# Value projection in blocks of four heads through DRAM, in place of blocks of two heads kept on chip, in a two-layer hybrid decoder

## The chip, the cores and the metric

The kernel runs on one core of one Trainium2 chip. The metric is the time of one execution in microseconds (us) on the device; lower is better.

## The reference

The input is x, 1024 tokens by 1024 channels, float32. Two residual layers follow, then a final RMSNorm; every layer is `x = x + mixer(rmsnorm(x))`.

```python
# layer 0: one projection u @ w_in, split into two branches
z, xBC, dt, q, k, v, g = split(u @ w_in)
xBC = silu(causal_dwconv(xBC))              # Mamba-2 branch: 4 groups, 8 chunks of 128 tokens
y_a = rmsnorm((ssd_scan(xs, dt, A, B, C) + xs * D_skip) * silu(z))
# differential attention: 8 heads, two softmax maps each, values 128 wide
w   = softmax(q0 k0 + bias) - lam * softmax(q1 k1 + bias)
y_b = rmsnorm(w @ v) * silu(g)
out = concat(y_a, y_b) @ w_out
# layer 1: gated recurrence (HGRN2), 16 heads of 128
q, f, i, g = split(u @ w_in)                # i are the values of the recurrence
o = gated_linear_recurrence(silu(q), 1 - f, i, log f)
out = (rmsnorm(o) * silu(g)) @ w_out
```

Layer 0 needs 1024 value columns (8 heads of 128), layer 1 needs 2048 (16 heads of 128).

## The kernel before, in words

Matrix products in float32 are made of three products of rounded parts: each operand is split into a high and a low part, and TensorE (PE in the profile) adds high·high, high·low and low·high in PSUM. The normed input of a layer, `u`, lies on chip for the whole layer, 8 high and 8 low tiles of 128 channels by 1024 tokens.

Weights come in blocks of 256 columns by 1024 rows (`wspecs` is the list of blocks in the order of their use). `_wprep` loads a block in two halves into `w_raw` on the SP queue (L126), rounds it on ScalarE (ACT, L132) into `w_hi`, and takes the rest on VectorE (DVE, L133) into `w_lo`. There are two buffers of each, so one block can be made ready while another is in use; `wnext` hands out a block and begins the next.

A projection comes in two forms. `mm_cm` (L174) has the weights stationary and streams 512 tokens per matmul; it makes queries, keys, gates and the scan's inputs. `mm_tm` (L184) has 128 tokens of `u` stationary and streams the weight columns, 256 per matmul; it makes the values, which are wanted with tokens on partitions, and the output projections. Both write a PSUM tile `pj`, of which there are two of one bank each. A `pj` tile is free for the next piece when ACT and DVE have taken its result out.

Values: `v_pieces` takes one weight block (two heads) and makes, in four pieces of 48 matmuls, the two tiles `V` that hold 1024 tokens by 256 value columns; ACT copies each piece out of PSUM (L199). The tag `V` has four buffers, so two pairs of heads fit.

Layer 0 first runs the scan group by group. The order of PE's instructions there is written out by `weave`: the projections of group g+1 are cut into pieces, and behind certain pieces the steps of group g's scan are put. Each of the 8 chunks has a `first` step (transposes; the decay matrix R, tile `G` or `wT`, read from DRAM on SP, L464, shifted on DVE, L482, exponentiated on ACT) and a `second` step two pieces later (L502 to L508). The numbers that `at` gives are the pieces behind which the steps come. In the last group there is no next group; the pieces are the query and key projection of attention head 0 (4), the values of heads 0 and 1 (4) and the gates (4).

Then come 8 attention heads, and in them and in all of layer 1 a scheduler orders each engine's instructions. A head has 8 query blocks i of 128 tokens. `soft(i)` makes two score maps of 128 by 128(i+1) in PSUM tiles `big` (L603), takes their maxima with the bias on DVE (L607 for the last 256 columns, L611 for the rest, L613), exponentials on ACT (L617), and combines the two maps on DVE (L621 to L624). `values(i)` transposes the result (L635, copies L637) and multiplies with `V` (L639). Queries and keys of a head are taken out of `pj` by ACT (L569) and DVE (L570) into `A` tiles; head h+1's are projected beside head h's work. Behind odd heads the next two heads' values are projected, before even heads their gates.

Layer 1 has 16 heads of the recurrence (`hgrn_core`); per head a projection of q and f, then before even heads the gates of two heads, after odd heads the values of the next two.

Of the kernel before, what the change touches and what calls it, by code (L numbers as in the profile page):

```python
# [89 lines left out]
class Net:  # L90
# [23 lines left out]
    def _wprep(self, i):  # L114
# [4 lines left out]
        hi = self.t("w_hi", [P, KT, WB], F32R)  # L119
        lo = self.t("w_lo", [P, KT, WB], F32R)  # L120
        for q in range(2):
            raw = self.t("w_raw", [P, KT // 2, WB])
            k0 = q * (KT // 2)
            o = 0
            for c0, n in cols:
                nc.sync.dma_start(  # L126
                    raw[:, :, o:o + n],
                    src[row0 + k0 * P:row0 + (k0 + KT // 2) * P, c0:c0 + n].rearrange(
                        "(k p) n -> p k n", p=P))
# [57 lines left out]

    def v_pieces(self, u, vs):
        nc = self.nc
        w = self.wnext()  # L190
        for q in range(2):
            v = self.t("V", [P, 4, WB])
            vs.append(v)
            for j2 in range(2):
                pj = self.ps("pj")
                for j in range(2):
                    sl = slice((q * 4 + j2 * 2 + j) * P, (q * 4 + j2 * 2 + j + 1) * P)
                    self.mm_tm(pj[:, j * WB:j * WB + WB], w, [x[:, sl] for x in u[0]], [x[:, sl] for x in u[1]])
                nc.scalar.copy(v[:, 2 * j2:2 * j2 + 2, :], pj.rearrange("p (t n) -> p t n", n=WB))  # L199
                yield  # L200
# [994 lines left out]
```

## Time and profile before

| | |
|---|---|
| median of 3 runs | 2237.67 us (2235.84 to 2238.94) |
| the profiled execution | 2242.69 us |
| its span in the profile | 2240.9 us, so 1.8 us lie outside |
| PE busy | 2178.8 us (97%), 16868 matmuls |
| DVE busy | 1269.9 us (57%) |
| ACT busy | 832.2 us (37%) |
| chain that ended last | PE 51%; first lines: pj L174 24%, pj L184 14% |
| DMA | 169.14 MB, mean 75 GB/s |
| granted TensorE clock, mean | 0.991 of full speed |

The profiled execution is 5.0 us longer than the median of the runs. A busy PE is not PE at its peak: each matmul's end is modelled, and two that follow each other overlap in the rows. The distance from start to start is what one costs.

### The profile page before, as it was taken

Reading aid. Unit: us, or ns where it says so; the run is one execution under the profiler, and the core shown is the slowest. Engines: PE = TensorE matmul, PEld = TensorE weight load, DVE = VectorE, ACT = ScalarE, POOL = GpSimd, SP = SyncE. Lnnn points to the kernel's source line nnn. Section 1 sums busy time; section 2 is a strip of 40 time slices with the busy share of each in tenths; the row PEclk is TensorE's granted clock in tenths of the full one; section 3 lists DMA queues with packets and bytes.
Section 4 is the critical chain, followed back from the end, with each engine's and each line's share of the span. In section 5 each row is a group of like instructions: output and inputs, shape, how many; then the busy total and the mean of one; then the engine's idle time right before and its main releaser. Section 6 shows DMA issues by size and latency. Waiting matters only on the chain.

```text
span 2240.9 us, 40897 instructions
## 1 busy us (share of the span) xinstructions
PE 2178.8 (97%) x16868; PEld 1920.3 (86%) x16868; DVE 1269.9 (57%) x2864; ACT 832.2 (37%) x1903; POOL 188.8 (8%) x216
## 2 busy tenths in 40 slices
PE   6998998899999999999999999999999999999998
PEld 5787776789898988999988989898989898989998
DVE  4765766565656556755453555555555555557444
ACT  4333333234444545644442323232323222324233
POOL 1001111110000000000010010101010101010000
PEclk9999999999999999999999999999999999999999
DMA  4322233332212221525331111111111111125333
GB/s 138 67 84 66 80 85 81 74 81 64 69 36 67 64 69 41 170 66 159 119 104 39 48 48 48 48 48 48 48 48 48 48 49 48 48 67 165 111 103 122
DMA packets 182256, 169.14 MB, mean 75 GB/s; under 512 B 10239, under 2 KB 163233, under 8 KB 182068
## 3 DMA queue, kind: packets, MB, share of 16 engines
q1 hardware_dynamic: 174564, 152.42, 23.1%
q0 software_dynamic: 3280, 9.90, 2.1%
q10 hardware_dynamic: 4224, 4.19, 0.6%
q8 instruction: 132, 2.16, 0.4%
q14 instruction: 56, 0.46, 0.1%
HBM read 132.66 MB, written 25.43 MB: 71 GB/s over the span
## 4 chain that ended last, share of the span: by engine, by line
PE 51%; DMA 1%; ACT 0%; DVE 0%; issue 0%; POOL 0%; POOLq 0%; ACTq 0%
PE pj L174 24%; PE pj L184 14%; PE big L184 5%; PE big L1051 2%; PE big L1139 1%; PE big L1141 1%; PE s L1128 1%; PE big L1093 1%; PE s L1155 1%; PE s L1122 1%; PE big L1087 0%; PE s L159 0%; DMA ey<-yb 0%; DMA th<-in_lvmask 0%; ACT w_hi L132 0%; DVE w_lo L133 0%
## 5 line engine op out<-in xcount | busy, mean ns | idle before, releaser
L174 PE MATMUL pj<-u,w_hi 128*128 128x512 f32 x3072 | 990.0, 400 | 31.3 <-DVE A L233 21.2
L174 PEld LDWEIGHTS pj<-u,w_hi 128*128 128x128 f32 x3072 | 573.4, 190 | 154.7 <-DVE A L233 23.0
L174 PE MATMUL pj<-u,w_lo 128*128 128x512 f32 x1536 | 607.9, 396 | 0.0
L184 PE MATMUL pj<-w_hi,u 128*128 128x256 f32 x2592 | 492.6, 286 | 1.0 <-DVE A L233 1.0
L184 PEld LDWEIGHTS pj<-w_hi,u 128*128 128x128 f32 x2592 | 409.9, 191 | 3.6 <-DVE A L233 1.4
L184 PE MATMUL pj<-w_lo,u 128*128 128x256 f32 x1296 | 368.3, 284 | 0.0
L174 PEld LDWEIGHTS pj<-u,w_lo 128*128 128x128 f32 x1536 | 291.8, 190 | 61.1 <-issue 0.2
L133 DVE TENSOR_TENSOR w_lo<-w_raw,w_hi 128x1024 fp32r<-128x1024 f32 x168 | 206.3, 1251 | 116.9 <-ACT w_hi L132 116.6
L184 PEld LDWEIGHTS pj<-w_lo,u 128*128 128x128 f32 x1296 | 247.8, 191 | 1.0
L132 ACT CAST w_hi<-w_raw 128x1024 fp32r<-128x1024 f32 x168 | 168.1, 1047 | 188.8 <-PE pj L174 107.6
L233 DVE SCALAR_TENSOR_TENSOR A<-th,pj 128x512 f32<-128x512 f32 x80 | 55.1, 689 | 140.9 <-ACT th L232 140.4
L232 ACT ACTIVATE th<-pj 128x512 f32<-128x512 f32 x96 | 57.2, 596 | 208.5 <-PE pj L174 190.8
L617 ACT ACTIVATE p<-p,mx 128x256 f32<-128x256 f32 (+7 forms) x128 | 98.5, 771 | 72.4 <-DVE mx L613 66.4
L148 POOL TENSOR_TENSOR ro<-rs_t,mhalf 128x4 f32<-128x4 f32 x48 | 52.8, 1100 | 682.4 <-DVE rs_t L147 489.1
L603 PE MATMUL big<-A 128*128 128x512 f32 (+3 forms) x384 | 90.3, 352 | 2.6 <-DMA A<-A 1.3
L968 POOL TENSOR_SCALAR A<-th,fN,fB 128x512 f32<-128x512 f32 x32 | 47.6, 1488 | 470.0 <-ACT th L965 470.0
L637 ACT COPY wT<-s 128x512 f32<-128x512 f32 (+2 forms) x96 | 45.8, 477 | 95.8 <-PE s L635 95.1
L639 PE MATMUL s<-V,wT 128*128 128x128 f32 x576 | 79.7, 275 | 0.6 <-ACT wT L637 0.6
L1035 DVE TENSOR_TENSOR A<-A,p 128x512 f32<-128x512 f32 x96 | 65.8, 686 | 23.5 <-PE big L1051 23.0
L639 PEld LDWEIGHTS s<-V,wT 128*128 128x128 f32 x576 | 74.4, 191 | 3.3 <-ACT wT L637 1.1
L1030 DVE TENSOR_TENSOR p<-p,p 128x512 f32<-128x512 f32 x96 | 66.2, 690 | 15.5 <-PE big L1087 6.2
L603 PEld LDWEIGHTS big<-A 128*128 128x128 f32 x384 | 64.5, 189 | 11.3 <-issue 2.3
(330 smaller groups left out, 2977.1 us busy)
## 6 DMA issues: line engine op xcount, KB each, us to landing
w_raw<-in_even_w_in SPq DMA_DIRECT2D x32, 512.0 KB, 4.7
w_raw<-in_odd_w_in SPq DMA_DIRECT2D x64, 256.0 KB, 3.3
w_raw<-in_odd_w_in SPq DMA_DIRECT2D x32, 512.0 KB, 3.9
w_raw<-in_even_w_in SPq DMA_DIRECT2D x48, 256.0 KB, 4.3
w_raw<-in_even_w_out SPq DMA_DIRECT2D x24, 512.0 KB, 4.4
w_raw<-in_odd_w_out SPq DMA_DIRECT2D x24, 512.0 KB, 4.6
A<-A POOLq DMA_DIRECT2D x32, 256.0 KB, 5.5
yo<-ey SPq DMA_DIRECT2D x32, 256.0 KB, 2.0
```

Source lines behind the costliest of these rows:

```text
L132: nc.scalar.copy(hq, raw)
L133: nc.vector.tensor_tensor(lq, raw, hq.bitcast(F32), op=ALU.subtract)
L148: return nc.gpsimd.tensor_tensor(dst, t[:, :n], self.mhalf[:, :n], op=ALU.pow)
L174: nc.tensor.matmul(out, lhsT=ww[:, k, ms], rhs=uu[k][:, sl], start=(n == 0), stop=(n == 3 * KT - 1))
L184: nc.tensor.matmul(out, lhsT=uu[k], rhs=ww[:, k, :], start=(k == 0 and j == 0), stop=(k == KT - 1 and j == 2))
L232: nc.scalar.activation(th, pj, AF.Tanh, scale=0.5)
L233: nc.vector.scalar_tensor_tensor(out, view(th), 1.0, view(pj), op0=ALU.add, op1=ALU.mult)
L603: nc.tensor.matmul(s[:, k0:k0 + kn], lhsT=q[:, isl], rhs=ks[j][:, k0:k0 + kn], start=(j == 0), stop=(j == 1))
L617: nc.scalar.activation(p[:, :n], p[:, :n], AF.Exp, bias=mx, accum_out=z)
L639: nc.tensor.matmul(po[:, i % 4, :], lhsT=wT[:, j * P:j * P + P], rhs=V(j, hh), start=(j == 0), stop=(j == i))
L1030: nc.vector.tensor_tensor(q, q, bc(t0, [P, L // (2 * h), h]), op=ALU.mult)
L1035: nc.vector.tensor_tensor(k, k, bc(halves(Ts[h], 1)[1], [P, L // (2 * h), h]), op=ALU.mult)
```

## The change

Values are projected for four heads at once. A value block is now two weight blocks of 512 rows by 512 columns, which together fill both weight buffers; a matmul streams 512 columns (L187). For each pair of 128-token tiles two `pj` tiles are filled: in the first and the last pair in the order tile 0 and tile 1 with the first weight block, then both with the second; in the others tile by tile. ACT copies a tile into a staging `V` tile of two token tiles, SP stores it to the DRAM tensor `v_d`, and `v_load` reads two tiles of 1024 tokens by 256 columns back for each pair of heads. Value blocks stand in layer 0 in the scan's last group (heads 0 to 3) and at head 3 (heads 4 to 7), in layer 1 at heads 0, 3, 7 and 11. Since a value block is now 8 pieces, the last scan group has 16 pieces, and its steps stand at 1.5 + 1.6c in place of 1.5 + c. Line numbers move: L174 is now L176, L184 is L187, L482 is L502, L570 is L590, L603 is L623, L635 is L655, L639 is L659.

```diff
 def _wprep(self, i):
...
-        hi = self.t("w_hi", [P, KT, WB], F32R)
-        lo = self.t("w_lo", [P, KT, WB], F32R)
+        wid = sum(n for _, n in cols)
+        kt = KT * WB // wid
+        hi = self.t("w_hi", [P, kt, wid], F32R)
+        lo = self.t("w_lo", [P, kt, wid], F32R)
...
-    def v_pieces(self, u, vs):
+    def v_pieces(self, u, v_d, hb):
         nc = self.nc
-        w = self.wnext()
+        i = self.wpos
+        self.wpos += 2
+        self._wprep(i)
+        self._wprep(i + 1)
+        ws = self.wtiles[i], self.wtiles[i + 1]
+        for t in range(0, NT, 2):
+            pas = [self.ps("pj") for _ in range(2)]
+            order = ((0, 0), (1, 0), (0, 1), (1, 1)) if t in (0, NT - 2) else ((0, 0), (0, 1), (1, 0), (1, 1))
+            for j, kq in order:
+                sl = slice((t + j) * P, (t + j) * P + P)
+                self.mm_tm(pas[j], ws[kq], *([x[:, sl] for x in z[4 * kq:4 * kq + 4]] for z in u),
+                           first=kq == 0, last=kq == 1)
+                if t == NT - 2 and j == 1:
+                    self._wprep(i + 2 + kq)
+                if kq == 1:
+                    if j == 0:
+                        v = self.t("V", [P, 2, 512])
+                    nc.scalar.copy(v[:, j], pas[j])
+                    if j:
+                        nc.sync.dma_start(v_d[t * P:(t + 2) * P, hb * 512:hb * 512 + 512].rearrange(
+                            "(t p) n -> p t n", p=P), v)
+                    yield
+    def v_load(self, v_d, pair):
+        vs = []
         for q in range(2):
             v = self.t("V", [P, 4, WB])
+            self.nc.sync.dma_start(v, v_d[q * 512:q * 512 + 512, pair * WB:pair * WB + WB].rearrange(
+                "(t p) n -> p t n", p=P))
             vs.append(v)
...
+    values = lambda c0, hb: [(W, r0, [(c0 + hb * 512, 512)]) for r0 in (0, 512)]
...
-                pieces = chain(att_pieces(S, u, nxt), S.v_pieces(u, vs), S.gate_pieces(u, ("G", "bt"), sg))
-                steps = ssd_steps(S, g, tiles, ya, lambda c: 1.5 + c, 2)
+                pieces = chain(att_pieces(S, u, nxt), S.v_pieces(u, v_d, 0), S.gate_pieces(u, ("G", "bt"), sg))
+                steps = ssd_steps(S, g, tiles, ya, lambda c: 1.5 + 1.6 * c, 2)
...
         elif h < 7:
-            Vn = S.proj_v(u)
+            if h == 3:
+                run(S.v_pieces(u, v_d, 1))
+            Vn = S.v_load(v_d, h // 2 + 1)
...
         elif h < 15:
-            Vn = S.proj_v(u)
+            if h % 4 == 3:
+                run(S.v_pieces(u, v_d, h // 4 + 1))
+            Vn = S.v_load(v_d, h // 2 + 1)
```

**Place 1: the beginning of the value block in the scan's last group.** PE before: `pj_3118` is the first piece of values (48 matmuls), `pj_3207` the second; the rows with `big` and `s1` between them are scan steps.

```order
L508 MATMUL big_3070<-G_2956,p0_2963 64x128 x4
...
L470 MATMUL s1_3085<-ident_71,A_2417 128x128
L184 MATMUL pj_3118<-w_hi_2869,u_76 128x256 [waits DVE_49,PE_49]
L184 MATMUL pj_3118<-w_lo_2870,u_76 128x256
...
L184 MATMUL pj_3118<-w_hi_2869,u_91 128x256
L502 MATMUL big_3168<-A_2418,p0_2963 128x128 [waits Activation_49]
...
L508 MATMUL big_3168<-G_3023,p0_3030 64x128 x4
...
L470 MATMUL s1_3191<-ident_71,A_2417 128x128
L184 MATMUL pj_3207<-w_hi_2869,u_76 128x256 [waits DVE_49,PE_49]
```

PE now: `pj_3100` and `pj_3101` are the first two token tiles; 12 matmuls of 512 columns with the first weight block go to each, then the second weight block (`w_hi_3090`) begins.

```order
L528 MATMUL big_3071<-G_2957,p0_2964 64x128 x4
L187 MATMUL pj_3100<-w_hi_2870,u_77 128x512 [waits DVE_49,PE_49]
L187 MATMUL pj_3100<-w_lo_2871,u_77 128x512
...
L187 MATMUL pj_3100<-w_hi_2870,u_88 128x512
L187 MATMUL pj_3101<-w_hi_2870,u_77 128x512 [waits DVE_49,PE_49]
L187 MATMUL pj_3101<-w_lo_2871,u_77 128x512
...
L187 MATMUL pj_3101<-w_hi_2870,u_88 128x512
L187 MATMUL pj_3100<-w_hi_3090,u_81 128x512 [waits Activation_49]
```

The second `pj` tile of the block is asked for after 12 matmuls of 512 columns now; before, after 48 of 256 columns and two scan steps.

DVE before, the same place: `pj_3041` is the last piece of the query and key projection, `G_3189` a decay matrix R that SP reads from DRAM.

```order
L570 SCALAR_TENSOR_TENSOR A_2992<-pj_3041,A_2992 64x512 [waits Activation_49]
L532 COPY o_3081<-big_3070 128x2x128 [waits DMAHW6_49,Activation_49]
L514 TENSOR_TENSOR p0_3030<-p0_2963,ph_511 128x256
L482 TENSOR_SCALAR G_3189<-G_3189,ph_510 128x128 [waits DMAHW6_49]
L480 TENSOR_TENSOR bt_3090<-s1_3085,triu_132 128x128 [waits Activation_49]
L482 TENSOR_SCALAR G_3189<-G_3189,ph_510 128x128 x3
L570 SCALAR_TENSOR_TENSOR A_2993<-pj_3041,A_2993 64x512 [waits Activation_49]
L485 TENSOR_TENSOR wT_3083<-wT_3083,bt_3090 128x512 [waits DVE_49]
```

DVE now: `pj_3024` is that last piece, and its second row (into `A_2994`) is what frees the bank for `pj_3101`; `G_3221` is the R.

```order
L590 SCALAR_TENSOR_TENSOR A_2993<-pj_3024,A_2993 64x512 [waits Activation_49]
L500 TENSOR_TENSOR p0_3060<-s1_3055,triu_133 128x128 [waits Activation_49]
L552 COPY o_3082<-big_3071 128x2x128 [waits DMAHW6_49,Activation_49]
L534 TENSOR_TENSOR p0_3060<-p0_2964,ph_512 128x256
L502 TENSOR_SCALAR G_3221<-G_3221,ph_511 128x128 [waits DMAHW6_49]
L502 TENSOR_SCALAR G_3221<-G_3221,ph_511 128x128 x3
L505 TENSOR_TENSOR G_3053<-G_3053,p0_3060 128x512 [waits DVE_49]
L590 SCALAR_TENSOR_TENSOR A_2994<-pj_3024,A_2994 64x512 [waits Activation_49]
```

In both lists the second take-out of that piece stands behind the rows on an R; now a multiplication with the R before (`G_3053`) stands ahead of it too.

**Place 2: attention head 4, query blocks 3 to 6.** PE before: `big` are score maps, `s1` the values' products, `pj_7109` and `pj_7159` pieces of the values of heads 6 and 7.

```order
L603 MATMUL big_6580<-A_6275,A_6215 128x512 [waits DVE_49,PE_49]
L603 MATMUL big_6580<-A_6335,A_6215 128x512
L184 MATMUL pj_7109<-w_hi_6859,u_84 128x256
...
L184 MATMUL pj_7109<-w_hi_6859,u_83 128x256
L639 MATMUL s1_6521<-V_5609,wT_6554 128x128 [waits Activation_49]
...
L603 MATMUL big_6605<-A_6274,A_6214 128x512 [waits DVE_49,PE_49]
...
L184 MATMUL pj_7109<-w_lo_6860,u_83 128x256
...
L184 MATMUL pj_7159<-w_lo_6860,u_78 128x256
L639 MATMUL s1_6521<-V_5609,wT_6596 128x128 [waits Activation_49]
...
L603 MATMUL big_6666<-A_6274,A_6214 128x512 [waits DVE_49]
...
L184 MATMUL pj_7159<-w_hi_6859,u_86 128x256
...
L603 MATMUL big_6713<-A_6274,A_6214 128x512 [waits DVE_49]
```

PE now, from query block 3 to the next projection (`pj_7315`, the third piece of head 5's queries and keys); pieces 1 and 2 of that projection are `pj_7255` and `pj_7284`, ahead of this stretch.

```order
L623 MATMUL big_6418<-A_6123,A_6063 128x512 [waits DVE_49,PE_49]
...
L623 MATMUL big_6429<-A_6124,A_6064 128x512 [waits DVE_49,PE_49]
...
L623 MATMUL big_6454<-A_6123,A_6063 128x512 [waits DVE_49,PE_49]
...
L659 MATMUL s1_6370<-V_5666,wT_6403 128x128 [waits Activation_49]
...
L623 MATMUL big_6467<-A_6124,A_6064 128x512 [waits DVE_49,PE_49]
...
L623 MATMUL big_6515<-A_6123,A_6063 128x512 [waits DVE_49]
...
L659 MATMUL s1_6370<-V_5666,wT_6485 128x128 [waits Activation_49]
...
L623 MATMUL big_6562<-A_6123,A_6063 128x512 [waits DVE_49]
...
L623 MATMUL big_6618<-A_6123,A_6063 128x512 [waits DVE_49,PE_49]
...
L623 MATMUL big_6631<-A_6124,A_6064 128x512 [waits DVE_49,PE_49]
...
L659 MATMUL s1_6546<-V_5666,wT_6593 128x128 x4
L176 MATMUL pj_7315<-u_77,w_hi_6708 128x512 [waits DVE_49]
```

From the last matmul of `pj_7284` to the first of `pj_7315` PE has no projection: 40 score matmuls (query blocks 2 to 7, both maps), 21 transposes of weights, 19 value products and 4 transposes of the tail lie between. DVE's rows that free `pj_7255` stand here:

```order
L644 SCALAR_TENSOR_TENSOR p0_6521<-p1_6534,rr_6541,p0_6521 128x768 [waits DVE_49]
L643 RECIPROCAL rr_6588<-z0_6573 128x1 [waits Activation_49]
L627 ISA p1_6581,mx_6580<-big_6575,cm_6315 128x256 [waits DVE_49,PE_49]
...
L631 ISA p1_6581,mf_6583<-big_6575,far_851 128x640
...
L590 SCALAR_TENSOR_TENSOR A_7253<-pj_7255,A_7253 64x512 [waits Activation_49]
L590 SCALAR_TENSOR_TENSOR A_7253<-pj_7284,A_7253 64x512 [waits Activation_49]
...
L633 TENSOR_SCALAR mx_6580<-mx_6580,mf_6583 128x1 [waits DVE_49]
L590 SCALAR_TENSOR_TENSOR A_7254<-pj_7255,A_7254 64x512 [waits DMASW2_49,DMASW1_49,Activation_49]
```

They stand behind the maxima of query block 6 (`big_6575`) and the combination of block 5 (`p0_6521`).

## Rows read from the trace of the kernel before

**Rows 1.** Windows: us, busy time and count per engine, granted clock, DMA.

```profile
480.00:860.00 380.00, 380.00 (x2297) 338.11 (x2296) 216.24 (x682) 185.80 (x456) 24.22 (x34) 1.00 0.23 57
860.00:910.00 50.00, 47.76 (x278) 41.33 (x277) 35.14 (x96) 27.61 (x61) 3.70 (x6) 0.97 0.34 91
1168.00:2040.00 872.00, 871.11 (x8235) 755.36 (x8236) 478.31 (x941) 262.00 (x652) 78.71 (x59) 1.00 0.17 51
```

**Rows 2.** Timeline, TensorE, layer 1: start, us, instruction (L184, 256 columns).

```profile
1242.63 0.40 PE L184 MATMUL pj<-w_hi,u 128*128 128x256 f32 x2
...
1246.23 0.28 PE L184 MATMUL pj<-w_hi,u 128*128 128x256 f32 x1
```

**Rows 3.** Timeline, TensorE, layer 0, scan stage (L174, 512 columns).

```profile
132.38 0.62 PE L174 MATMUL pj<-u,w_hi 128*128 128x512 f32 x2
...
136.49 0.62 PE L174 MATMUL pj<-u,w_hi 128*128 128x512 f32 x2
```

**Rows 4.** Waits of TensorE from 390 to 410 us: total, times, longest.

```profile
PE pj L174 <- DVE A L570: 8.0, 1, 8.0
```

**Rows 5.** Window behind that wait, columns as in rows 1.

```profile
406.00:410.00 4.00, 4.00 (x11) 3.08 (x11) 0.03 (x1) 0.00 (x0) 0.95 (x2) 0.51 0.10 33
```

**Rows 6.** Timeline, SP queue (DMA issues), beginning of the value block in layer 0.

```profile
420.43 0.37 SPq L464 DMA_DIRECT2D G<-acs_d  x1
```

**Rows 7.** Timeline, VectorE, the same place.

```profile
426.66 0.29 DVE L482 TENSOR_SCALAR G<-G,ph 128x128 f32<-128x128 f32 x1 [2.09 <-DMA G<-acs_d]
...
427.77 0.69 DVE L570 SCALAR_TENSOR_TENSOR A<-pj,A 64x512 fp32r<-64x512 f32 x1
```

**Rows 8.** Timeline, TensorE, the same place.

```profile
420.89 0.36 PE L184 MATMUL pj<-w_hi,u 128*128 128x256 f32 x1
...
428.85 0.36 PE L184 MATMUL pj<-w_hi,u 128*128 128x256 f32 x1
```

**Rows 9.** DMA issues of the page: count, KB, median us to landing.

```profile
w_raw<-in_odd_w_in SPq DMA_DIRECT2D x32, 512.0 KB, 3.9
...
G<-acs_d SPq DMA_DIRECT2D x22, 256.0 KB, 4.9
```

**Rows 10.** Windows, attention head 4, value block (L184) alone.

```profile
764.00:792.00 28.00, 20.26 (x155) 19.14 (x154) 1.00 0.27 67
```

**Rows 11.** Groups of VectorE, 460 to 905 us: busy us, mean ns.

```profile
L570 DVE SCALAR_TENSOR_TENSOR A<-pj,A 64x512 fp32r<-64x512 f32 x55 | 37.9, 689 | 26.2 <-ACT A L569 25.2
...
L607 DVE CUSTOM_DVE_ANT_0 p<-big,cm 128x256 f32<-128x256 f32 x42 | 17.5, 421 | 15.8 <-PE s L635 14.6 <-PE big L603 1.1
L613 DVE TENSOR_SCALAR mx<-mx,mf 128x1 f32<-128x1 f32 x72 | 12.5, 208 | 0.2
...
L607 DVE DVE_READ_ACCUMULATOR2_ANT mx<- 128x1 f32 x98 | 8.1, 83 | 0.0
...
L611 DVE CUSTOM_DVE_ANT_0 p<-big,far 128x640 f32<-128x640 f32 x12 | 9.8, 820 | 0.0
...
L624 DVE SCALAR_TENSOR_TENSOR p<-p,rr,p 128x768 f32<-128x768 f32 x6 | 6.1, 1019 | 0.2
...
L624 DVE SCALAR_TENSOR_TENSOR p<-p,rr,p 128x384 f32<-128x384 f32 x6 | 3.7, 619 | 0.2
...
L611 DVE CUSTOM_DVE_ANT_0 p<-big,far 128x128 f32<-128x128 f32 x12 | 3.4, 286 | 0.0
```

**Rows 12.** Windows in attention head 5, columns as in rows 1.

```profile
880.00:888.00 8.00, 6.41 (x40) 5.33 (x38) 7.31 (x18) 3.91 (x9) 1.67 (x3) 0.99 0.35 82
861.00:892.00 31.00, 28.78 (x151) 24.15 (x151) 23.25 (x67) 16.48 (x39) 2.67 (x4) 0.94 0.25 73
```

**Rows 13.** Timeline, TensorE, in that stretch (values, 128 columns).

```profile
882.35 1.50 PE L639 MATMUL s<-V,wT 128*128 128x128 f32 x12
```

**Rows 14.** Costliest groups of the page: busy us, mean ns, idle before.

```profile
L133 DVE TENSOR_TENSOR w_lo<-w_raw,w_hi 128x1024 fp32r<-128x1024 f32 x168 | 206.3, 1251 | 116.9 <-ACT w_hi L132 116.6
...
L132 ACT CAST w_hi<-w_raw 128x1024 fp32r<-128x1024 f32 x168 | 168.1, 1047 | 188.8 <-PE pj L174 107.6
```

More of the change, by code (lines that the diff above doesn't have):

```diff
@@ L176, in mm_cm, with mm_tm @@
                 n += 1
-    def mm_tm(self, out, w, uh, ul, ks=range(KT)):
+    def mm_tm(self, out, w, uh, ul, first=None, last=None, ks=None):
         nc = self.nc
         wh, wl = w
-        for k in ks:
+        kt = KT if ks else len(uh)
+        for k in ks or range(kt):
             for j, (uu, ww) in enumerate(((uh, wh), (uh, wl), (ul, wh))):
-                nc.tensor.matmul(out, lhsT=uu[k], rhs=ww[:, k, :],
-                                 start=(k == 0 and j == 0), stop=(k == KT - 1 and j == 2))
@@ L188, in v_pieces @@
-    def v_pieces(self, u, vs):
+                nc.tensor.matmul(out, lhsT=uu[k], rhs=ww[:, k, :], start=(first is not False and k == 0 and j == 0),
+                                 stop=(last is not False and k == kt - 1 and j == 2))
+    def v_pieces(self, u, v_d, hb):
         nc = self.nc
-        w = self.wnext()
+        i = self.wpos
[20 more added lines that the diff above has]
+                    yield
@@ L191, in v_pieces @@
+    def v_load(self, v_d, pair):
+        vs = []
         for q in range(2):
             v = self.t("V", [P, 4, WB])
+            self.nc.sync.dma_start(v, v_d[q * 512:q * 512 + 512, pair * WB:pair * WB + WB].rearrange(
+                "(t p) n -> p t n", p=P))
             vs.append(v)
[L194 to L200, printed above, removed]
+        return self.v_of(vs)
@@ L807, in wspecs @@
         if h == 0:
-            specs.append((W, 0, [(AV0, WB)]))
+            specs += values(AV0, 0)
         if h % 2 == 0:
             specs.append((W, 0, [(AG0 + h * P, WB)]))
-        elif h < 7:
-            specs.append((W, 0, [(AV0 + (h + 1) * P, WB)]))
+        elif h == 3:
+            specs += values(AV0, 1)
     out = lambda w: [(w, half * D, [(cb * WB, WB)]) for half in (0, 1, 1) for cb in range(4)]
@@ L819, in wspecs @@
         if h == 0:
-            specs.append((W, 0, [(HI0, WB)]))
+            specs += values(HI0, 0)
         if h % 2 == 0:
             specs.append((W, 0, [(HG0 + h * P, WB)]))
-        elif h < 15:
-            specs.append((W, 0, [(HI0 + (h + 1) * P, WB)]))
+        elif h % 4 == 3 and h < 15:
+            specs += values(HI0, h // 4 + 1)
     return l0, specs + out(WO)
@@ L887, in layer0 @@
     yb = S.dram.tile([8, P, L], F32, name="yb")
+    v_d = S.dram.tile([L, D], F32, name="v_d")
     u = norm_first(S, x, lambda S: S.norm_c[:, 0:8])
@@ L918, in layer0 @@
         if h == 0:
-            V = Vn = S.v_of(vs)
+            V = Vn = S.v_load(v_d, 0)
         else:
@@ L938, in layer1 @@
     yo = S.dram.tile([16, P, L], F32, name="yo")
+    v_d = S.dram.tile([L, 2 * D], F32, name="v1_d")
     dgm = S.t("ph", [P, 256])
@@ L972, in layer1 @@
         if h == 0:
-            V = Vn = S.proj_v(u)
+            run(S.v_pieces(u, v_d, 0))
+            V = Vn = S.v_load(v_d, 0)
         if h % 2 == 0:
```

14 lines of the change are left out of this document (5 added, 9 removed).

## Prediction

> **What bounds the kernel now.** I read the windows first, because the mean share of PE hides that the stages differ. From 480 to 860 us PE is busy 380.00 of 380.00 us, and in layer 1 from 1168 to 2040 us 871.11 of 872.00 [rows 1]. In both DVE and ACT have much room. So in those stretches the time is the sum of what PE has to issue: a matmul made cheaper comes off the end whole, and a wait put into PE's order goes onto the end whole. From 860 to 910 us PE misses 2.2 us while DVE is busy 35.14 of 50 [rows 1]; that is the one attention stretch in which DVE shows through.
>
> **What the wide matmul saves.** A busy time says nothing about the price of a matmul, since neighbours overlap in the rows; start to start does. Ten triples of 256 columns take 1246.23 − 1242.63 = 3.60 us (the rows between repeat), 120 ns each [rows 2]. Six triples of 512 columns take 136.49 − 132.38 = 4.11 us, 228 ns each [rows 3]; single triples among them take 0.68 us, 227 ns. One wide matmul in place of two narrow ones saves 240 − 228 = 12 to 13 ns. Before there are 12 value blocks of 192 narrow matmuls, now 6 blocks of 192 wide ones: 1152 × 12 to 13 ns = 13.4 to 15.4 us. I take **−14.5 us**, in both layers alike.
>
> The rows for 512 columns are of the form with the weights stationary; the form with tokens stationary has none of that width, and I assume that it costs the same. By the Trainium skill ("TensorE: Matmul & The Clock Gate", section "Back-to-back issue gap") an isolated stream is spaced by the columns at 2.4 GHz and 2.5 ns more, so about 109 ns for 256 columns and 216 for 512. By that rule the saving would be some 2.5 ns per wide matmul, about 3 us in all, and the sum below some 11 us higher. The rows of this kernel show 120 and 228, so the trace does not agree with it.
>
> **What is unchanged.** Half blocks of weights rounded and split: 24 for the values before and after (6 blocks of two weight blocks of two halves). ACT takes 48 tiles of 128 by 512 out of PSUM, as before. The scan's steps are the same, set further apart.
>
> **The trip through DRAM.** It adds 24 stores of 512 KB and 24 loads of 512 KB. A transfer of that size lands in 3.9 us [rows 9], so some 8 us from the last copy to the values on chip. Layer 0's first block has the gates behind it (96 matmuls, 22 us), layer 1's first too, and the later ones are wanted a head later. The cover is 22 us or more, so the price is nothing; with the cover gone it would be 8 us a block. A staging tile may wait for a store, about 4 us, but PE needs 48 × 0.228 = 10.9 us for the next pair of tiles. On SP the added issues stand among weight loads that have a whole block's time; the DMA share in layer 1 is 0.17 [rows 1].
>
> **Place 1, the beginning of the value block in the scan.** PE already waits once close by, 8.0 us for a take-out of `pj` by DVE [rows 4], and then runs at the lower of its two clock levels (1.2 of 2.4 GHz): granted 0.51, 11 matmuls in 4.00 us [rows 5], where at 228 ns they take 2.5, so 1.5 us lost. Now the same sort of wait can come again. In the trace SP issues the read of R at 420.43 [rows 6]; DVE is idle for it until 426.66 and ends the second take-out of the last query and key piece at 427.77 + 0.69 = 428.46 [rows 7], 8.0 us after the issue. PE begins values at 420.89 and asks for that bank at 428.85 [rows 8], 0.4 us after it came free. In the new order the second bank is asked for after 12 × 0.228 = 2.7 us, and the value block begins about 0.1 us before the R's issue, because the four transposes between now stand elsewhere. DVE has one more 0.69 us multiplication ahead of the take-out and one of 0.28 less: done 8.4 us after the issue, asked for 2.6 us after it, so a wait of 5.8. If the read is seen after its usual 4.9 us [rows 9] and not after the 6.2 of that trace, 4.5. If the issue comes earlier against PE than I read, less: 3 at the low end, and nothing in the case that DVE is done in time. I take **+5.0**, and **+1.4** for the clock behind it.
>
> **Place 2, attention head 4.** Before, 192 narrow matmuls were spread through this head: from 764 to 792 us alone 20.26 of 28.00 us of PE are theirs [rows 10], and PE never stops. Now values for heads 4 to 7 are made beside head 3, and from query block 2 to 6 of head 4 no projection stands in PE's order; the third piece of head 5's queries and keys waits until DVE has taken out the first, and that stands behind the maxima of block 6. So this stretch runs at DVE's pace. DVE, per block i and map: 0.42 for the near columns, two read-outs of 0.08, 0.21 to join the maxima, and the far columns, 0.29 for 128 and 0.82 for 640, so 0.13 per 128; per block the combination, 0.62 for 384 and 1.02 for 768, and three small ones of about 0.2 [rows 11]. Blocks 2, 3, 4, 5: 3.3, 3.7, 4.1, 4.5; the maxima of 6: 3.2; three take-outs of 0.69; two tail operations of 512 columns, 1.4. Sum 22.3 us. PE in it: 40 score matmuls with 16,896 columns at 120 ns per 256, 7.9 us, and 44 of 128 columns, of which the 19 value products run twice, 63 at 0.12 (12 in 1.50 us [rows 13]), 7.6; together 15.5. In the one stretch of before where DVE sets the pace it is busy 7.31 of 8.00 us, over a longer stretch 23.25 of 31.00 [rows 12]. At the first share 22.3 takes 24.4 us and PE stands idle for 9; at the second 29.7, idle for 14. At the low end DVE does block 2 beside the projection before it and never pauses: 19.0 − 15.5 = 3.5. I take **+9.0**, the first share, since DVE has a full queue there, and **+1.5** for the half clock behind it (nothing to 2.5).
>
> **Handing over the weights.** A value block holds both weight buffers, so its second weight block can be rounded only when the block before has left its buffer, and the next weights only at the last pair. A half takes 1.05 us on ACT and 1.25 on DVE [rows 14], 2.3 together; the order in the first and last pairs gives PE 24 wide matmuls, 5.5 us, before it needs the first half. That covers it when ACT and DVE come at once; both are often in the midst of something of 1 to 3 us. I take **+1.0** for all six blocks, between nothing and 4.
>
> **Sum.** −14.5 + 5.0 + 1.4 + 9.0 + 1.5 + 1.0 = +3.4 us. Against the profiled execution, 2242.69, that is 2246.1; the median of the runs is 5.0 us shorter than the profiled one, so the forecast for the median is 2237.67 + 3.4 = **2241.1 us**. A difference under 0.2%, 4.5 us, can't be told from no change: same is from 2233.2 to 2242.1.
>
> **Rivals.** (a) The waits are hidden. DVE runs ahead through head 4, the idle there is 3.5 us, R lands before PE asks: −14.5 + 3.5 + 0.4 = −10.6, **2227**. For it: DVE is busy only 216 of 380 us in attention [rows 1]. Against: those 57% are with a projection to fill; the sums above are of one stretch. It decides if place 2 idles under 5 us and place 1 under 1. (b) Slower by one mechanism: the weight handover misses in each of the five later blocks by about 3 us, because ACT's rounding stands behind a projection's take-outs: +15 in place of +1, **2255**. For it: ACT's rounding sat idle 107.6 us in all waiting for PE's `pj` [rows 14], so buffers come free late. Against: 5.5 us cover a 2.3 us step. It decides from a cover lost of about 2 us. (c) Both places at their upper ends: 14 + 2.5 and 5.8 + 2, with 2 for the weights, −14.5 + 26.3 = +11.8, **2249**. (d) The wide form with tokens stationary takes 237 ns, not 228, and saves 3 ns each: −3.5 in place of −14.5, **2252**. The rule of the Trainium skill cited above comes to about the same. Against: 228 with another stationary operand per matmul in rows 3.
>
> **Chances.** Forecast, 2235 to 2246: 0.40. (a) 0.29, (b) 0.10, (c) 0.16, (d) 0.05. Faster by over 0.2%: nearly all of (a) and a little of the forecast, 0.30. Same: the forecast below 2242.1 and the rest of (a), 0.30. Slower: what is left of the forecast, 0.09, and (b), (c), (d), 0.40. The range goes from (a) to 2253; it leaves out (b) and the tails, under 2 in 10: **2227 to 2253**. The forecast alone holds 2235 to 2246.
>
> **What the new profile would show.** The saving: wide value matmuls 227 to 229 ns from start to start. Place 1: PE waiting some 5 us for DVE L590 at the second `pj` tile, with a granted clock of a half behind it. Place 2: about 25 us in head 4 without L176, PE idle near 9 us, mostly waiting for DVE, and DVE nearly full. Layer 1: no wait over 1 us on `w_lo` or `w_hi`, and a stage shorter by 4 × 2.4 = 9.7 us. Wrong would be: PE busy throughout head 4; waits on weights at each block; PE waiting for `V` from DRAM.

## The result and the profile after

The changed kernel takes 2272.16 us in the median of four runs (2268.85 to 2278.52), the kernel before on the same chip 2238.31 (2235.84 to 2244.93): a ratio of 1.0152, 95% interval 1.0138 to 1.0167. It is 34 us slower. The forecast was 2241.1, its range ended at 2253.

The page of the kernel after, span and busy time of each engine:

```profile
span 2268.9 us, 38708 instructions
...
PE 2184.7 (96%) x15716; PEld 1866.6 (82%) x15716; DVE 1265.1 (56%) x2864; ACT 834.0 (37%) x1903; POOL 191.6 (8%) x216
```

PE issues 1152 matmuls fewer than before and is busy 5.9 us longer (2178.8 us before). The span grew by 28.0 us, so idle time grew too. To see where, both traces are cut at two marks that stand in both: the first instruction of the scan's last group and the first score of layer 1; the third mark is the end of layer 1's last head. Windows of the kernel before, layer 0 from the scan's last group on, then the heads of layer 1 (columns as in rows 1):

```profile
395.80:1158.80 763.00, 748.78 (x5017) 683.45 (x5015) 439.25 (x1247) 356.48 (x848) 54.36 (x78) 0.99 0.31 85
1158.80:2102.30 943.50, 942.48 (x9026) 823.10 (x9026) 520.20 (x1023) 284.21 (x711) 85.23 (x66) 1.00 0.18 57
```

The same two stages, and in the last row the stretch of attention head 4 without a projection, in the kernel after:

```profile
390.20:1176.60 786.40, 754.80 (x4630) 668.11 (x4628) 440.77 (x1249) 355.39 (x848) 55.12 (x78) 0.98 0.34 93
1176.60:2130.40 953.80, 946.83 (x8258) 787.98 (x8258) 516.20 (x1025) 287.54 (x712) 85.97 (x66) 1.00 0.23 74
...
810.48:837.65 27.17, 21.05 (x112) 16.90 (x110) 19.78 (x79) 17.33 (x57) 2.86 (x4) 0.87 0.24 69
```

Layer 0's stage is 23.4 us longer, layer 1's 10.3. The rest, where the two programs are alike, is 5.7 us shorter; nearly all of that lies ahead of the first mark, in a part that is the same in all kernels here and took 389.8 to 398.8 us in their profiled executions, so it is not the change's. In layer 0 idle time of PE went from 763.00 − 748.78 = 14.2 to 31.6 us, in layer 1 from 1.0 to 7.0. PE's busy time rose in both, though by the forecast each should have fallen by 2.4 us per wide value block.

Waits of TensorE in the kernel after, layer 0's stage (total, times, longest):

```profile
PE pj L176 <- DVE A L590: 10.4, 3, 8.0
PE pj L187 <- DVE A L590: 6.3, 1, 6.3
PE big L528 <- DVE G L505: 5.0, 1, 5.0
```

The first answers to [rows 4]. The second is place 1 of the prediction; the read of R, VectorE's take-out and TensorE's next matmul there, in the kernel after:

```profile
414.87 0.37 SPq L484 DMA_DIRECT2D G<-acs_d  x1
...
423.21 0.69 DVE L590 SCALAR_TENSOR_TENSOR A<-pj,A 64x512 fp32r<-64x512 f32 x1
...
424.05 0.77 PE L187 MATMUL pj<-w_hi,u 128*128 128x512 f32 x1 [6.28 <-DVE A L590]
```

The third was not foreseen; it comes in attention head 0, while the scan's last chunk is still woven in. Timeline of SP's queue there, in the kernel after:

```profile
489.41 7.43 SPq L610 DMA_DIRECT2D ph<-tz_d  x6
496.94 0.38 SPq L484 DMA_DIRECT2D G<-acs_d  x1
```

The read of R for the last chunk (L484, the line that [rows 6] show as L464) stands on SP behind six loads of head 1's bias rows. Their issues alone take 0.3 to 0.6 us each, 2.6 in all; most of the 7.43 us is a wait in the queue (waits of SP from 480 to 500 us, same columns as above):

```profile
SPq L610 <- DMA V<-v_d: 4.5, 1, 4.5
```

The third of the six waits until the second of two reads of the values back from DRAM has landed; both tell of their landing by the same semaphore. That read was issued at 484.39 and took 10.4 us, where the median of the 24 in this kernel is 3.9; the DMA share is 0.69 or more in every 2 us from 484 to 496. So the trip through DRAM has a part in this wait. VectorE has nothing else to do for 8.3 us:

```profile
501.62 0.87 DVE L502 TENSOR_SCALAR G<-G,ph 128x128 f32<-128x128 f32 x4 [8.28 <-DMA G<-acs_d]
503.24 0.69 DVE L505 TENSOR_TENSOR G<-G,p 128x512 f32<-128x512 f32 x1 [0.74 <-ACT G L504]
```

TensorE begins the chunk's last products only at 503.99:

```profile
503.99 1.12 PE L528 MATMUL big<-G,p 128*64 128x128 f32 x8 [4.99 <-DVE G L505]
```

Windows behind place 1's wait and behind this one, kernel after. Both show PE at the lower of its two levels (1.2 GHz) after it had stood still for 5 to 6 us:

```profile
424.00:428.40 4.40, 4.35 (x10) 3.47 (x11) 0.00 (x0) 0.00 (x0) 0.00 (x0) 0.50 0.54 117
504.00:508.00 4.00, 4.00 (x15) 3.09 (x16) 3.32 (x11) 0.78 (x3) 0.00 (x0) 0.50 0.14 31
```

In layer 1 no wait on weights shows at all. Waits of TensorE there, kernel after:

```profile
PE pj L176 <- DVE A L253: 4.1, 3, 1.4
PE big L1169 <- DVE bt L1162: 1.2, 1, 1.2
PE pj L187 <- DVE A L253: 1.0, 1, 1.0
```

**Where layer 1's busy time went.** Before, a value block stood behind each odd head up to 13; now one stands behind heads 3, 7 and 11 alone. Behind heads 1, 5, 9 and 13 only the next head's queries and forget gates (22 us) are left for PE to interleave with the core of the head; I call these heads bare. Groups of TensorE in layer 1's stage, kernel before (count | busy us, mean ns | idle before):

```profile
L1051 PE MATMUL big<-A 128*32 128x48 f32 x3072 | 46.2, 208 | 0.0
L1141 PE MATMUL big<-bt,p 128*128 128x128 f32 x224 | 43.5, 276 | 0.0
```

and the same two, scores and state products, in the kernel after:

```profile
L1079 PE MATMUL big<-A 128*32 128x48 f32 x3072 | 54.7, 209 | 0.7 <-ACT A L1066 0.7
...
L1169 PE MATMUL big<-bt,p 128*128 128x128 f32 x224 | 46.4, 289 | 1.2 <-DVE bt L1162 1.2
```

The counts are equal, the busy time is 8.5 and 2.9 us more. Busy time is not what they cost, since neighbours overlap in it. Counted from each start to the next, idle time left out, the scores take 41.8 us before and 48.2 after, the two products of the output 52.1 and 57.9, all small matmuls together 15.6 us more; the projections take 11.3 us less, and idle time is 6.0 us more: together the 10.3. The timelines show how. In a bare head of the kernel after, the scores and the two products stand in turns:

```profile
1519.06 0.54 PE L1079 MATMUL big<-A 128*32 128x48 f32 x28
1519.52 0.49 PE L1169 MATMUL big<-bt,p 128*128 128x128 f32 x2
1519.85 0.39 PE L1167 MATMUL big<-V,G 128*128 128x128 f32 x2
1520.16 0.36 PE L1079 MATMUL big<-A 128*32 128x48 f32 x10
1520.45 0.49 PE L1169 MATMUL big<-bt,p 128*128 128x128 f32 x2
```

In the kernel before, the same products run in one piece beside a projection:

```profile
1478.40 0.39 PE L1141 MATMUL big<-bt,p 128*128 128x128 f32 x2
1478.62 0.39 PE L1139 MATMUL big<-V,G 128*128 128x128 f32 x2
1478.85 0.39 PE L1141 MATMUL big<-bt,p 128*128 128x128 f32 x2
...
1481.08 0.39 PE L1141 MATMUL big<-bt,p 128*128 128x128 f32 x2
```

Before, four products take 1478.85 − 1478.40 = 0.45 us; after, 1520.16 − 1519.52 = 0.64, and the ten scores 0.29. The turn thus holds some 0.2 us that the products did not need before. Where 28 scores stand in a row they take 1519.52 − 1519.06 = 0.46: 18 more scores cost 0.17 us, some 10 ns each, so about 0.19 us comes with a row of scores, however short it is.

Over all starts in this stage a row of scores (scores that follow each other with nothing between) takes 0.17 us and 10 ns for each score. The matmul just ahead of the row takes 0.09 us longer than in a row of its own kind, the one just behind it 0.10. So each row costs 0.36 us beside its scores. Before there are 62 such rows, after there are 97: 35 × 0.36 = 12.6 us, and with 6.0 us of idle time 18.6 of the 20 us between the forecast −9.7 and the measured +10.3.

### The profile page after: what moved, and what is told of

Read it like the earlier page. It is cut to its first block, busy times and chain, and to the rows that moved or that the text cites. A ratio compares the mean times of both kernels' runs of the same rounds, so it can differ in the third digit from the quotient of the medians.

```text
span 2268.9 us, 38708 instructions
## 1 busy us (share of the span) xinstructions
PE 2184.7 (96%) x15716; PEld 1866.6 (82%) x15716; DVE 1265.1 (56%) x2864; ACT 834.0 (37%) x1903; POOL 191.6 (8%) x216
## 4 chain that ended last, share of the span: by engine, by line
PE 85%; DMA 6%; DVE 5%; ACT 2%; issue 1%; POOL 0%; SPq 0%; POOLq 0%; ACTq 0%; DVEq 0%
PE pj L176 43%; PE pj L187 19%; PE big L187 6%; PE big L623 2%; PE s L659 2%; PE big L1079 2%; DMA G<-acs_d 1%; PE big L1169 1%; PE s L655 1%; PE big L1167 1%; DMA wT<-acs_d 1%; PE s L1156 1%; DMA w_raw<-in_even_w_in 1%; PE big L1121 1%; PE s L1183 1%
## 5 line engine op out<-in xcount | busy, mean ns | idle before, releaser
L176 PE MATMUL pj<-u,w_hi 128*128 128x512 f32 x3072 | 986.0, 399 | 37.1 <-DVE A L253 24.9
L176 PEld LDWEIGHTS pj<-u,w_hi 128*128 128x128 f32 x3072 | 572.0, 190 | 160.5 <-DVE A L253 27.1
L176 PE MATMUL pj<-u,w_lo 128*128 128x512 f32 x1536 | 607.5, 396 | 0.0
L187 PE MATMUL pj<-w_hi,u 128*128 128x256 f32 (+1 forms) x1824 | 446.1, 332 | 7.3 <-DVE A L590 6.3
L187 PEld LDWEIGHTS pj<-w_hi,u 128*128 128x128 f32 x1824 | 311.3, 190 | 39.3 <-issue 7.2
L176 PEld LDWEIGHTS pj<-u,w_lo 128*128 128x128 f32 x1536 | 291.2, 190 | 60.7 <-issue 0.2
L187 PE MATMUL pj<-w_lo,u 128*128 128x256 f32 (+1 forms) x912 | 301.9, 331 | 0.0
L187 PEld LDWEIGHTS pj<-w_lo,u 128*128 128x128 f32 x912 | 173.7, 190 | 14.8
L623 PE MATMUL big<-A 128*128 128x512 f32 (+3 forms) x384 | 92.1, 358 | 3.0 <-DVE mf L631 1.2
L659 PE MATMUL s<-V,wT 128*128 128x128 f32 x576 | 81.3, 278 | 1.9 <-ACT wT L657 1.8
L659 PEld LDWEIGHTS s<-V,wT 128*128 128x128 f32 x576 | 75.8, 194 | 6.2 <-ACT wT L657 3.5
L623 PEld LDWEIGHTS big<-A 128*128 128x128 f32 x384 | 65.6, 192 | 13.3 <-issue 2.4
L1066 ACT COPY A<-p 128x256 f32<-128x256 f32 x128 | 46.2, 410 | 72.0 <-DVE p L1058 71.5
```

What stands on the lines that cost most here:

```text
L176: nc.tensor.matmul(out, lhsT=ww[:, k, ms], rhs=uu[k][:, sl], start=(n == 0), stop=(n == 3 * KT - 1))
L187: nc.tensor.matmul(out, lhsT=uu[k], rhs=ww[:, k, :], start=(first is not False and k == 0 and j == 0), stop=(last is not False and k == kt ...
L623: nc.tensor.matmul(s[:, k0:k0 + kn], lhsT=q[:, isl], rhs=ks[j][:, k0:k0 + kn], start=(j == 0), stop=(j == 1))
L659: nc.tensor.matmul(po[:, i % 4, :], lhsT=wT[:, j * P:j * P + P], rhs=V(j, hh), start=(j == 0), stop=(j == i))
```

## The experiments

The theories, as the expectations name them. **G** (gathered): the wide blocks gather what filled eight places into four, and the heads left bare cost more than the matmuls save. **P** (places): the two waits of layer 0 cost more than forecast, layer 1 is as forecast. **W** (weights): the handover of the weight buffers misses. **D** (DRAM): storing and reading the values back costs time.

**One layer at a time.** l1_only has layer 0 as before and layer 1 as after; l0_only is the other way round. l1_only against the kernel after (l0_only does the same to layer 1's lines):

```diff
@@ wspecs, layer 0
-            specs += values(AV0, 0)
+            specs.append((W, 0, [(AV0, WB)]))
...
-        elif h == 3:
-            specs += values(AV0, 1)
+        elif h < 7:
+            specs.append((W, 0, [(AV0 + (h + 1) * P, WB)]))
@@ layer0
...
-                steps = ssd_steps(S, g, tiles, ya, lambda c: 1.5 + 1.6 * c, 2)
+                steps = ssd_steps(S, g, tiles, ya, lambda c: 1.5 + c, 2)
...
-            if h == 3:
-                run(S.v_pieces(u, v_d, 1))
-            Vn = S.v_load(v_d, h // 2 + 1)
+            Vn = S.proj_v(u)
```

> Layer 0 as before, layer 1 as in the change. Theory G (gathered work: value blocks gathered at every fourth head leave other heads with too little projection beside them): layer 1 loses about 21 us to waits and changes of matmul kind and saves 10 to 11, so about 10 us over before, 2248. Theory D (the trip through DRAM and the SP queue): nearly all of the loss sits in layer 0, where a read of R came late behind the added transfers; layer 1 then keeps its saving, 2228. Theory W (weight handover): about 3 us at each of three later blocks, PE waiting for w_hi or w_lo, 2236 to 2238.

> Layer 0 as in the change, layer 1 as before. Theory G: the rest of the loss, 22 to 26 us over before, 2260 to 2264; with the run above the two add up to the change's 34. Theory D: the whole 34 or more, 2272 to 2280. Theory W: one later block only, so little, 2238 to 2245.

Measured against 2240.46 us before: l1_only 2254.46, ratio 1.0067 (1.0044 to 1.0090), so +14.0; l0_only 2261.07, 1.0100 (1.0074 to 1.0125), so +20.6. They add up to 34.6, the whole of the 33.9 between the medians. Layer 1 alone is slower, where the forecast had a gain of 9 and G 10 us of loss.

**The same places with narrow matmuls.** narrow4 keeps the gathered blocks, the 16 pieces and the trip through DRAM, but each pair of heads has its own weight block and matmuls of 256 columns.

```diff
-    values = lambda c0, hb: [(W, r0, [(c0 + hb * 512, 512)]) for r0 in (0, 512)]
+    values = lambda c0, hb: [(W, 0, [(c0 + hb * 512 + p * WB, WB)]) for p in range(2)]
...
```

> As the change in the places of the value blocks, the 16 pieces and the trip through DRAM, but with two weight blocks of 256 columns one after the other, matmuls of 256 columns and the usual handing on of weights. Theory G: the saving of 14.5 us is gone and the losses of the gathering stay, so about 2272 + 14 = 2286. Theory W: handover losses go too, so 2240 to 2252. Theory D: as G here, 2286.

Measured: 2272.01, ratio 1.0144 (1.0129 to 1.0160), what the kernel after takes, and what no theory had said. Windows of narrow4, the two stages:

```profile
389.80:1167.20 777.40, 755.37 (x5018) 687.87 (x5019) 440.08 (x1248) 355.41 (x848) 55.25 (x78) 0.98 0.34 94
1167.20:2130.80 963.60, 955.33 (x9025) 829.27 (x9025) 513.83 (x1023) 285.85 (x711) 88.17 (x66) 1.00 0.23 73
```

The equal totals are a coincidence of two differences. Layer 1 is 9.8 us longer than in the kernel after: that is what the width saves there, 9.7 by the forecast. Against before it is 20.1 longer, the price of gathering with nothing to set against it (the trip costs nothing there, see the next run). Layer 0 is 9.0 us shorter than in the kernel after: its waits at place 1 and for R are 2.6 and 0.3 us in place of 6.3 and 5.0.

**The trip alone.** trip is the kernel before with each pair's values stored to DRAM and read back.

```diff
+                if j2:
+                    nc.sync.dma_start(v_d[q * 512:q * 512 + 512, pair * WB:pair * WB + WB].rearrange(
+                        "(t p) n -> p t n", p=P), v)
...
-            Vn = S.proj_v(u)
+            Vn = S.proj_v(u, v_d, h // 2 + 1)
```

> The kernel before, with each pair's values stored to DRAM and read back (24 stores and 24 loads of 512 KB), nothing else changed: same blocks, same places, 256 columns. Theory G: the trip is hidden, 2236 to 2243. Theory D: SP's order holds up reads of R and the near bias, so 2245 to 2265. Theory W says nothing here, 2238.

Measured: 2241.90 against 2240.46, ratio 1.0007 (0.9995 to 1.0019); layer 1's stage takes 943.50 us as before. D falls as the cause of the 34 us; its part in one wait of layer 0 is told above.

**Values left out of layer 1.** l1_bare is the kernel before without the value blocks behind heads 1 to 13 of layer 1; all its heads use the values of heads 0 and 1.

```diff
-        elif h < 15:
-            specs.append((W, 0, [(HI0 + (h + 1) * P, WB)]))
...
-        elif h < 15:
-            Vn = S.proj_v(u)
```

> The kernel before with the value blocks behind heads 1 to 13 of layer 1 left out: all its heads use the values of heads 0 and 1 (this part of the work is not done). Seven blocks of 192 narrow matmuls go, 23.7 us each in the trace of before, 166 us. If a block costs what its matmuls take, the time falls by 166 us to about 2073. Theory G: a head that loses its value block loses 5 to 7 us to waits and to changes between its small matmuls, so seven give back 42 less: a fall of 117 to 131, 2108 to 2122.

Measured: 2109.48 against 2237.45, 128.0 us less, ratio 0.9427 (0.9399 to 0.9454). Windows of layer 1's heads in l1_bare:

```profile
1154.90:1968.50 813.60, 800.84 (x7683) 671.58 (x7682) 494.29 (x1009) 258.68 (x669) 82.29 (x66) 1.00 0.18 56
```

Seven blocks of 192 matmuls at 120 ns are 161 us; the stage fell by 943.5 − 813.6 = 129.9. So 31 us came back, 4.5 us for each of the seven heads made bare: 11.7 of the 31 as idle time, the rest as slower small matmuls (113 rows of scores in place of 62, 51 × 0.36 = 18.4 us). Groups of TensorE in the same stage of l1_bare:

```profile
L1047 PE MATMUL big<-A 128*32 128x48 f32 x3072 | 58.9, 209 | 0.2 <-ACT A L1034 0.2
L1137 PE MATMUL big<-bt,p 128*128 128x128 f32 x224 | 47.9, 296 | 0.4 <-DVE bt L1130 0.4
```

The same two groups grow as in the kernel after, with no wide matmul, no gathered block and no trip through DRAM in the program. This is G's mechanism by itself.

**Layer 1 with its work spread again.** In l1_half each wide block is made in two token halves, one behind each odd head up to 11; layer 0 is as before.

```diff
-            if h % 4 == 3:
-                run(S.v_pieces(u, v_d, h // 4 + 1))
+            if h < 12:
+                t0 = h % 4 // 2 * 4
+                run(S.v_pieces(u, v_d, (h + 3) // 4, t0, t0 + 4))
```

> Layer 0 as before. Layer 1 with the wide matmuls and the trip through DRAM, but after the first block each block of four heads is projected in two halves of 512 tokens, one behind each odd head up to 11, so that every head but the last has about as much projection beside it as before; the weights are loaded and rounded once for each half. Theory G: the loss of the gathering goes, apart from the bare last heads (about 4 us), and 10 us are saved, so 2230 to 2236. If the loss in layer 1 comes from the width itself (long matmuls between the small ones) or from the weight handover, which now comes six times and not three, it stays or grows: 2252 to 2262.

Measured: 2238.63 against 2239.61, ratio 0.9999 (0.9988 to 1.0010): the loss is gone, but the gain that G forecast did not come. Windows of layer 1's heads in l1_only and in l1_half:

```profile
1154.70:2110.80 956.10, 948.84 (x8258) 789.63 (x8258) 516.10 (x1023) 286.60 (x711) 86.36 (x66) 1.00 0.23 73
1150.70:2095.00 944.30, 940.62 (x8257) 783.89 (x8257) 531.37 (x1035) 298.04 (x723) 88.63 (x66) 1.00 0.26 81
```

With head 13 still bare the stage takes 944.3 us, 11.8 less than the 956.1 of l1_only. l1_mix makes the values of heads 2 to 13 in wide halves, those of heads 0, 1, 14 and 15 narrow, and spreads the last over heads 11 and 13, so that no head up to 13 is bare:

```diff
+            if h < 10:
+                run(S.v_pieces(u, v_d, 256 + (h + 1) // 4 * 512, *((4, 8) if h % 4 == 1 else (0, 4))))
+            else:
+                S.v_narrow(u, v_d, 7, (h - 11) // 2)
```

> Layer 0 as before. Layer 1: values of heads 2 to 13 in three wide blocks, each in two halves of tokens (at heads 0, 1, 3, 5, 7 and 9), heads 0 and 1 and heads 14 and 15 narrow, the latter in two halves at heads 11 and 13, so that no head is without value work. Theory G: the 7 us lost at the bare last heads in the halves run become 2 to 4, and three blocks save about 2.5 us each; 2233 to 2237 against 2240 of before. If the loss of the halves run has another cause, it stays: 2239 to 2243.

Windows of layer 1's heads in l1_mix:

```profile
1154.40:2094.60 940.20, 939.18 (x8451) 792.46 (x8450) 535.52 (x1037) 298.98 (x725) 87.85 (x66) 1.00 0.25 80
```

PE stands idle 1.0 us as before, and the stage is 3.3 us shorter than before. The median, 2237.95 against 2238.52, ratio 0.9996 (0.9986 to 1.0006), can't be told from no change and is 1 us above the range of G. So spreading the work takes away the loss; a gain that counts did not come of it.

The rows of scores say why. For each kernel: rows of scores in layer 1; 0.36 us for each row over the 62 of before; idle time over before; what the wide or missing blocks take off; the sum of the three; and the stage as measured, against before:

| | rows | rows' cost | idle | blocks | sum | measured |
|---|---|---|---|---|---|---|
| l1_mix | 71 | 3.2 | 0.0 | −7.3 | −4.1 | −3.3 |
| l1_half | 81 | 6.8 | 2.7 | −9.7 | −0.2 | +0.8 |
| narrow4 | 95 | 11.9 | 7.3 | 0 | 19.2 | +20.1 |
| kernel after | 97 | 12.6 | 6.0 | −9.7 | 8.9 | +10.3 |
| l1_only | 97 | 12.6 | 6.3 | −9.7 | 9.2 | +12.6 |
| l1_bare | 113 | 18.4 | 11.7 | −161.3 | −131.2 | −129.9 |

The sums come within 1.4 us, in l1_only within 3.4. This is read from traces; no run sets the number of rows by itself.

**The waits of layer 0, one by one.** Each of these is l0_only with one edit. l0_tile makes the first pair of token tiles one after the other, so that the second bank is asked for later. l0_bias issues the bias loads of heads 0 and 1 from GpSimd's queue. l0_spread sets the scan's steps one piece apart in place of 1.6. l0_g3only makes heads 4 to 7 as before, narrow, behind heads 3 and 5. In this order:

```diff
-            order = ((0, 0), (1, 0), (0, 1), (1, 1)) if t in (0, NT - 2) else ((0, 0), (0, 1), (1, 0), (1, 1))
+            order = ((0, 0), (1, 0), (0, 1), (1, 1)) if t in cross else ((0, 0), (0, 1), (1, 0), (1, 1))
...
-                pieces = chain(att_pieces(S, u, nxt), S.v_pieces(u, v_d, 0), S.gate_pieces(u, ("G", "bt"), sg))
+                pieces = chain(att_pieces(S, u, nxt), S.v_pieces(u, v_d, 0, (NT - 2,)), S.gate_pieces(u, ("G", "bt"), sg))
```

```diff
-        nc.sync.dma_start(near[16 * i:16 * i + 16],
+        (nc.gpsimd if h < 2 else nc.sync).dma_start(near[16 * i:16 * i + 16],
```

```diff
-                steps = ssd_steps(S, g, tiles, ya, lambda c: 1.5 + 1.6 * c, 2)
+                steps = ssd_steps(S, g, tiles, ya, lambda c: 1.5 + c, 2)
```

```diff
-            if h == 3:
-                run(S.v_pieces(u, v_d, 1))
-            Vn = S.v_load(v_d, h // 2 + 1)
+            Vn = S.proj_v(u) if h > 1 else S.v_load(v_d, 1)
```

> Layer 0 as in the change, layer 1 as before, but the first pair of tiles in the scan's last group goes tile by tile, so the second pj tile is asked for after 24 wide matmuls (5.5 us) and not 12. Theory P (the 6.3 us wait is the take-out of the last query and key piece coming late): the wait falls by 2.7 to about 3.6 us, 2 to 4 us less than the 2261 of the change of layer 0 alone. If PE waits for the weights of the second block there instead, the wait stays: 2261.

> Layer 0 as in the change, layer 1 as before, but the bias loads of heads 0 and 1 go through GpSimd's queue and not SP's. If the read of R for the last chunk is late because SP still issues those loads when its buffer comes free, the 4.5 to 5 us wait of PE for the product with R goes, and some half clock: 4 to 7 us less than 2261. If the added stores and loads of the values hold SP up, the wait stays.

> Layer 0 as in the change, layer 1 as before, and the scan's last steps put back to 1.5 + c. The change of layer 0 alone took 2261. If the spread over 16 pieces is what lets the read of R for the last chunk come behind the next head's bias loads, the wait of 4.5 to 5 us and its half clock go: 2253 to 2256. If that read is late because of the added transfers alone, no change: 2259 to 2263. The wait for the second pj tile (6.3 us) stays by either.

> Layer 0 with the wide block for heads 0 to 3 in the scan's last group, but heads 4 to 7 in two narrow blocks behind heads 3 and 5 as before; layer 1 as before. Theory G: head 4's stretch has its projection again, so its 6 us of idle and the half clock go, while the 2.5 us of the second wide block are lost; 2261 becomes 2254 to 2257. If the scan's last group is the whole of layer 0's loss: 2262 to 2264.

Waits of TensorE from 380 to 530 us in l0_tile:

```profile
PE pj L176 <- DVE A L609: 8.2, 1, 8.2
PE big L547 <- DVE G L524: 3.5, 1, 3.5
PE pj L187 <- DVE A L609: 2.6, 1, 2.6
```

Place 1's wait is 2.6 us in place of 6.3, by the order of two tiles alone. The same stretch in l0_bias:

```profile
PE pj L176 <- DVE A L609: 8.2, 1, 8.2
PE pj L187 <- DVE A L609: 6.0, 1, 6.0
```

The wait for R's chain (4.5 us in l0_only) is gone once the bias loads stand in another queue, and the stage takes 779.2 us in place of l0_only's 786.8 (l0_tile's takes 781.3). In l0_spread it is gone too, and the stage takes 783.3; in l0_g3only head 4's stretch has no idle time, but head 2 to 3 has 4.0 us, and the stage takes 782.8. So each wait has the cause that its edit names. The medians, 2257.11, 2261.91, 2259.98 and 2264.60 against l0_only's 2261.07, don't separate: four runs of one of these kernels lie up to 12 us apart, and the part ahead of the first mark took 390.9 to 398.8 us in the profiled executions of these four. By its median only l0_tile met its forecast; l0_bias, l0_spread and l0_g3only lie 4 to 8 us above theirs, the last just above the 2262 to 2264 of its rival, that the scan's last group is the whole loss of layer 0. Against that rival stands its trace alone. What each wait is worth is known from the traces, one profiled execution of each kernel.

## Why the prediction was wrong

**The step that failed** is the first one: "a matmul made cheaper comes off the end whole", applied to layer 1 as −9.7 us. It reckoned what 768 wide matmuls cost and not what the small ones cost when their neighbours move away. For attention head 4 the prediction asked which projection stands beside the core; for layer 1's heads it did not, though the same edit empties four of them. Layer 1 came out at +10.3 by the traces, 20.0 us above the −9.7. Four bare heads at the 4.5 us of l1_bare are 18, narrow4 gives 20.1 for gathering without width, and 35 more rows of scores with 6.0 us more idle time are 18.6. The forecast took PE busy for PE at its peak: in the kernel after it is busy 946.83 of 953.80 us and slower than before.

**The wide matmul** was right. Timeline of place 1's value block, kernel after:

```profile
437.11 0.63 PE L187 MATMUL pj<-w_hi,u 128*128 128x512 f32 x2
...
441.23 0.62 PE L187 MATMUL pj<-w_hi,u 128*128 128x512 f32 x2
```

Six triples take 4.12 us, 229 ns each, as forecast from [rows 3]. By the rule for an isolated stream in the Trainium skill that the prediction cited ("TensorE: Matmul & The Clock Gate", section "Back-to-back issue gap") it would be some 216; the trace does not agree. Rival (d), 237 ns, falls.

**Place 1**: 6.3 us for 5.0, by the chain given: R issued at 414.87, DVE's take-out at 423.21, PE on at 424.05. DVE was done 423.21 + 0.69 − 414.87 = 9.0 us after the issue, where the prediction had 8.4. At a granted clock of 0.50 for 4.4 us the half clock cost 2.2, not 1.4.

**Place 2**: L176 is absent from 810.48 to 837.65, 27.2 us where about 25 were named; PE is idle 27.17 − 21.05 = 6.1 us, not 9, and at a clock of 0.87 loses up to 3.5 more, not 1.5. Together up to 9.6 for 10.5. DVE "nearly full" was wrong: it is busy 19.78 of 27.17 us, and PE's waits are many short ones, the longest 1.1 us. So the chain from engine to engine seems to pace this stretch, not DVE's sum; no run tried this.

**Not priced in layer 0**: the R read behind the bias loads, one of which waited for the values to come back from DRAM: 5.0 us and 2.0 for the clock. The prediction looked at this read where the value block begins and not at where the wider spacing would put the chunk after it. With the three waits, 17.4 us of idle time, the half clocks, 7.7, and the saving of 4.8, the stage comes to +20.3; measured are +23.4 by the traces, +20.6 by l0_only's median. Some 3 us by the traces are not located.

**Handover of the weights**: 1.0 was forecast, no wait on `w_lo` or `w_hi` shows in layer 1. Rival (b) falls, and with it W. **The trip**: forecast 0, by itself measured 0 within the interval; in the kernel after its late landing holds up SP's queue for 4.5 us. Rival (a) falls. (c) priced its two places at 24.3 us, where the traces show 18.1, and its 2249 is refuted too, since it kept layer 1's gain and had no third wait.

**Open**: why a change into or out of a row of scores costs what it does was read from timelines and not tried by itself. l1_only's layer 1 is 2.3 us longer than the same layer in the kernel after. narrow4's layer 0 still loses 14.4 us with its waits short, 7.8 of them as idle time. None of this was followed up.

## What to carry to other kernels

Where a stage is bound by PE, list for every piece of small, dependent work which long projection stands beside it, before and after; a gather that makes the projection cheaper and empties places costs these places their filler, here 4.5 to 5 us each against 2.4 us saved per block. A busy share near 100% does not say that PE is at its peak: compare, from start to start, groups whose count did not change, and count in how many rows they stand. When steps are spaced further apart, follow each one's DMA issue in its queue to the new place, and see what stands ahead of it there and what that itself waits for.

## What was not expected of the hardware

Matmuls of equal shape and count cost more by their neighbours alone: 3072 scores took 41.8 us from start to start before, 48.2 after and 51.6 in l1_bare, at a granted clock of 1.00 in all three. It goes by rows: 62, 97 and 113 of them, each 0.17 us beside some 10 ns per score, and 0.19 more in the matmuls next to it. Six small loads with 2.6 us of issue held back by 7.4 us a read for which VectorE stood idle, because one of them waited 4.5 us in the queue for an earlier transfer to land, and TensorE lost 2 us more at half its clock after its wait.
